# Dispatch of several experts' tokens in one product on split rows, in two groups of places

## The chip, the cores and the metric

The kernel runs on one core of one Trainium2 chip. The metric is the device time of one execution in microseconds (us). TensorE is called PE in the profile, VectorE DVE, ScalarE ACT, GpSimd POOL, SyncE SP.

## What is computed

Two transformer blocks in float32 on a sequence of 256 tokens with 1024 features. The change lies in the last layer of the second block, a mixture of experts: a router picks 2 of 8 experts for each token, each expert is a gated network with 3584 hidden features, and the results are weighted and added to their tokens.

```python
D_MODEL = 1024; SEQ = 256; N_EXPERTS = 8; TOP_K = 2; EXPERT_FF = 7 * D_MODEL // 2

def swiglu(h, w_gate, w_up, w_down):
    return (jax.nn.silu(h @ w_gate) * (h @ w_up)) @ w_down

def moe_swiglu(h, w_router, w_gate, w_up, w_down):
    xt = h.reshape(-1, D)
    logits = (xt @ w_router).astype(jnp.float32)
    top_logit, top_idx = lax.top_k(logits, TOP_K)
    gates = jax.nn.softmax(top_logit, axis=-1)
    ...
    xs = xt_pad[tok_buf].reshape(n_blocks, EXPERT_BLOCK, D)
    def expert_block(args):
        xb, e = args
        return swiglu(xb, w_gate[e], w_up[e], w_down[e])
    ys = lax.map(expert_block, (xs, block_expert)).reshape(rows, D)
    ys = ys * gate_buf[:, None].astype(ys.dtype)
    out = jnp.zeros((T + 1, D), ys.dtype).at[tok_buf].add(ys)[:T]
```

## The kernel before

Everything ahead of the experts' layer (attention, convolution, two feed-forward networks) takes the first 753 us and is the same code in both kernels. Dense products there split a float32 operand into two rounded parts of type fp32r, high and low (H and L; `evac_hl`: ACT copies the rounded part, DVE subtracts it from the source), and multiply part by part.

In the experts' layer the 8 places e = 0 to 7 are worked one after the other. Which expert takes which place is decided on the chip by its count of tokens (`places`); places 1, 4 and 7 (`SMALL`) hold up to 64 tokens, the others (`MID`) up to 96 (`CAP`). A place goes through 7 steps d. `gate_up` multiplies the tokens' features (32 or 64 columns of the array, plain float32) with four pieces of weights of 1 MB, `turn` makes silu(gate) times up on ACT and DVE and transposes it on PE (tile `hT`), and `down` multiplies it with two more pieces of 1 MB. `gu` and `gv` are the banks of gate_up, `yb` those of down. Weights come in one stream over SP's DMA queue into a ring of buffers: 8 `raw`, 4 `more0` to `more3` (`EXTRA`), one of two 512 KB halves (`more`, `gn`) and six of two halves (`late`), 19 pieces of 1 MB. A buffer is asked for again as soon as PE has read it (`done`, `issue`).

The tokens of a place are gathered by a product, `dispatch(e)`: `one_hot` writes for each half t of the 256 tokens a 128x128 matrix (token against slot) into the tile `co`, and for each of the 8 blocks of 128 features the normalised rows `z` (tile `xTL`, plain float32) are the stationary operand and the one-hot the moving one, CAP columns wide (64 or 96). Four blocks share a bank `ga`, and ACT copies it to `plain(e)` (tile `xTH`). `back(e)` transposes the one-hot for `combine`, which scatters the results later. Place 0 is dispatched ahead of the loop, from the slots that the router's chain on DVE has just made; the other places in steps that are pushed between weight products: `under` runs one step of the list `aside` at the third and the sixth of the eight blocks of a `gate_up`. `prepare(e + 1)` joins the list after `gate_up` of d = 4. Within these rules a scheduler orders the instructions of each engine.

Of the kernel before, what the change touches and what calls it, by code (L numbers as in the profile page):

```python
# [15 lines left out]
D = 1024  # L16
# [84 lines left out]
EXTRA = 4  # L101
# [15 lines left out]
def build(tc, ap, dbg=None):  # L117
# [1113 lines left out]
    with tc.tile_pool(name="moe", bufs=1) as p:  # L1231
        z = zt
        pad(p, "moe")
        ex = [wide(tag, F32R, E_OFF).rearrange("p (i c s) -> p i c s", i=2, c=8) for tag in ("xTH", "xTL")]
        for i in range(EXTRA):
            issue([p.tile([128, HALF], F32, name="more%d" % i, tag="more%d" % i)])
        pl = wide("xTH", F32)
# [14 lines left out]
        def plain(e):  # L1252

            return pl[:, e % 2 * 768:e % 2 * 768 + 8 * CAP[e]].rearrange("p (c s) -> p c s", c=8)
# [12 lines left out]
        def dispatch(e):  # L1267
            n = CAP[e]
            per = 4
            for b in range(8 // per):  # L1270
                ps = mmbank("ga")
                for i in range(per):
                    cs = slice((per * b + i) * 128, (per * b + i + 1) * 128)
# [3 lines left out]
                o = slice(per * b, per * b + per)  # L1277
                psv = ps[:, 0:per * n].rearrange("p (c s) -> p c s", c=per)
                if e in SMALL + MID:
                    nc.scalar.activation(out=plain(e)[:, o, :], in_=psv, func=AF.Copy)  # L1280
                else:
                    evac_hl(ex[e % 2][:, 0, o, :], ex[e % 2][:, 1, o, :], psv)
                yield
# [9 lines left out]
        def flat(e):  # L1293
            return [ex[e % 2][:, i].rearrange("p c s -> p (c s)") for i in range(2)]

        def combine(e, yb, OHT):
            yH, yL = flat(e)
            n = 128
            if e in SMALL:

                evac_hl(yH[:, 0:512], yL[:, 0:512], yb[0])
            elif e in MID:
                n = CAP[e]
                y = p.tile([128, D], F32, name="y", tag="y", bufs=1)
# [9 lines left out]
            else:  # L1314
                for h in range(2):
                    cs = slice(h * 512, (h + 1) * 512)
                    evac_hl(yH[:, cs], yL[:, cs], yb[h])
# [15 lines left out]

        warm(AF.Silu, rsz[:, 1:2])
        one_hot(0)
        drain(dispatch(0))
# [72 lines left out]
        def prepare(e):  # L1409
            one_hot(e)  # L1410
            yield
            yield from dispatch(e)
            ohts[e] = back(e)
            yield

        def first():
            ohts[0] = back(0)
            yield
            gates()
            yield  # L1420
            places()
            yield

        def hidden(e, d, dt, i=0):

            n = CAP[e]
            if d == 6:
                w = pl[:, 1536:] if dt is F32 else flat(e)[i]
                return w[:, 0:4 * n].rearrange("p (c s) -> p c s", c=4)
            return p.tile([128, 4, 128], dt, name=("hH", "hL")[i], tag=("hH", "hL")[i], bufs=1)[:, :, 0:n]  # L1430

# [4 lines left out]
        def gate_up(e, d, pc):  # L1436
            n = CAP[e]
            if n == 128:
                eH, eL = ex[e % 2][:, 0], ex[e % 2][:, 1]
                ps = [mmbank("gu") for _ in range(2)]  # L1440
                for k8 in range(8):
                    for c in range(2):
                        if 2 * k8 + c in (UG, UG + 7):
                            under()
                        wh, wl = pc(k8 * 1024 + c * 512, 512)
                        mm3(ps[c], eH[:, k8, :], eL[:, k8, :], wh, wl, k8 == 0, k8 == 7)
                return ps
# [27 lines left out]
        def turn_of(e, d, ps, hs):  # L1475

            n = CAP[e]
            if n == 128:
                ss_ = [sb[:, c] for c in range(2)]
                for c in range(2):  # L1480
                    gated(ps[c], ss_[c], 256)
            else:
                ss_ = [sb[:, 0]]
                gated(ps[0], ss_[0], 256)
                if n == 96:
                    ss_.append(sb[:, 1, 0:128])
                    gated(ps[1], ss_[1], 128)

            def turn():
# [6 lines left out]
                if n == 128:  # L1496
                    hH, hL = hidden(e, d, F32R), hidden(e, d, F32R, 1)
                    evac_hl(hH, hL, hT.rearrange("p (c s) -> p c s", c=4))
                    hs[d] = (hH, hL)
                    return  # L1500
                h = hidden(e, d, F32)
# [12 lines left out]
        def down(e, d, pc, h, yb):  # L1514
            n = CAP[e]
            if n == 128:
                hH, hL = h
                order = [(kt, c) for kt in range(4) for c in range(2)]
                if d == 6:
                    order.sort(key=lambda o: o[1])  # L1520
                for m, (kt, c) in enumerate(order):
                    if m == UD:
                        under(0)
                    wh, wl = pc(kt * 1024 + c * 512, 512)
                    mm3(yb[c], hH[:, kt, :], hL[:, kt, :], wh, wl, d == 0 and kt == 0, d == 6 and kt == 3)
                return
# [40 lines left out]
        def overflow(e, beyond):  # L1567
# [11 lines left out]
            y = m[:, D:2 * D]  # L1579
            for b in range(2):  # L1580
                ps = mmbank("ga")
                for i in range(4):
                    cs = slice((4 * b + i) * 128, (4 * b + i + 1) * 128)
                    for t in range(2):
                        nc.tensor.matmul(ps[:, i * 128:(i + 1) * 128], z[:, t, cs], OH[:, t, :], start=t == 0,
                                         stop=t == 1)
                nc.vector.tensor_copy(out=eo[:, 4 * b:4 * b + 4, :], in_=ps.rearrange("p (c s) -> p c s", c=4))
            yb = [accbank("yb") for _ in range(2)]
            for d in range(7):
# [15 lines left out]
                hs_ = p.tile([128, 4, 128], F32, name="hso", tag="hH", bufs=1)  # L1605
# [9 lines left out]
            for h in range(2):  # L1615
                nc.scalar.activation(out=y[:, h * 512:(h + 1) * 512], in_=yb[h], func=AF.Copy)
            for t in range(2):
                for h in range(2):
                    cs = slice(h * 512, (h + 1) * 512)
                    ps = mmbank("cb")  # L1620
                    nc.tensor.matmul(ps, OHT[:, t * 128:(t + 1) * 128].bitcast(F32), y[:, cs], start=True, stop=True)
# [171 lines left out]
```

## Time and profile before

| | us |
|---|---|
| median of 3 runs | 1624.11 |
| lowest and highest run | 1623.15, 1629.3 |
| the profiled execution, its own time | 1626.53 |
| its span in the trace | 1624.5 |

The profile shows the profiled execution alone. Its own time is 2.0 us over its span and 2.4 us over the median of the runs. An engine's busy time is the union of its instructions; matmuls overlap, so the spacing of their starts tells their cost, not the duration of one. A plain float32 matmul leaves two records in the trace, an fp32r matmul one.

### The profile page before, as it was taken

How to read it: one execution, taken by the hardware profiler on the slowest of the kernel's cores; microseconds unless marked ns; L12 is line 12 of the kernel's file. 1: busy time of each engine (PE TensorE's matmuls, PEld its weight loads, DVE VectorE, ACT ScalarE, POOL GpSimd, SP SyncE). 2: the span in 40 equal slices, each digit the busy share in tenths (PEclk: the TensorE clock that was granted, in tenths of full speed). 3: DMA queues.
4: the chain of work that ended last, by engine and by line, in shares of the span. 5: the costliest groups of instructions: out<-in, count | busy, mean ns of one | idle time of the engine just before them, and what ended most of it. 6: DMA issues, size and time to landing. Idle time of an engine off the chain costs nothing.

```text
span 1624.5 us, 30626 instructions
## 1 busy us (share of the span) xinstructions
PE 1581.2 (97%) x12854; PEld 961.9 (59%) x12854; DVE 613.0 (38%) x1206; ACT 479.9 (30%) x879; POOL 21.9 (1%) x36
## 2 busy tenths in 40 slices
PE   7999999999999999999999999999999999999997
PEld 5879998877899998775343333443433334434332
DVE  6776555678555557972201011011011010110111
ACT  6655444667644446651101000010010000100100
POOL 0000000000000000010000000000000000000000
PEclk9999999999999999999999999999999999999999
DMA  9555555541555555238999999999999999999993
GB/s 380 217 191 201 189 198 182 194 156 53 182 202 187 182 182 195 69 137 340 415 380 374 416 416 414 415 417 401 379 370 415 418 418 415 415 388 387 357 417 127
DMA packets 86132, 478.81 MB, mean 295 GB/s; under 512 B 9761, under 2 KB 10529, under 8 KB 44770
## 3 DMA queue, kind: packets, MB, share of 16 engines
q1 hardware_dynamic: 83312, 468.58, 74.4%
q0 software_dynamic: 2240, 7.60, 1.4%
q8 instruction: 103, 1.69, 0.4%
q10 hardware_dynamic: 434, 0.59, 0.1%
q14 instruction: 43, 0.35, 0.1%
HBM read 475.03 MB, written 1.05 MB: 293 GB/s over the span
## 4 chain that ended last, share of the span: by engine, by line
PE 91%; DVE 5%; ACT 2%; issue 1%; DMA 0%; POOL 0%; SPq 0%; DVEq 0%; ACTq 0%; POOLq 0%
PE gu L1459 24%; PE yb L1534 12%; PE gv L1463 7%; PE acc L276 4%; PE acc L274 4%; PE acc L275 4%; PE yb L1539 4%; PE mm L276 3%; PE mm L274 3%; PE mm L275 2%; PE ga L1275 2%; PE hT L1494 2%; PE mm L297 2%; PE mm L296 2%; PE mm L295 2%; PE pg L297 1%
## 5 line engine op out<-in xcount | busy, mean ns | idle before, releaser
L226 DVE TENSOR_TENSOR wl<-raw,wh 128x1024 fp32r<-128x1024 f32 (+1 forms) x240 | 265.3, 1115 | 156.3 <-ACT wh L225 152.0
L225 ACT ACTIVATE wh<-raw 128x1024 fp32r<-128x1024 f32 (+1 forms) x240 | 230.8, 972 | 175.6 <-PE acc L276 64.1
L1459 PE MATMUL gu<-raw,xTH 128*32 128x512 f32 (+1 forms) x1240 | 190.0, 594 | 0.0
L1472 ACT ACTIVATE sm<-gu 128x256 f32<-128x256 f32 x56 | 21.5, 384 | 538.9 <-PE gu L1459 538.9
L1473 DVE TENSOR_TENSOR sm<-sm,gu 128x256 f32<-128x256 f32 x56 | 23.6, 421 | 384.4 <-ACT sm L1472 384.4
L1459 PE MATMUL gu<-late,xTH 128*32 128x512 f32 (+1 forms) x880 | 135.4, 595 | 0.0
L1459 PE MATMUL gu<-more,xTH 128*32 128x512 f32 (+1 forms) x708 | 107.6, 594 | 0.0
L1459 PEld LDWEIGHTS gu<-raw,xTH 128*32 128x32 f32 (+1 forms) x1240 | 49.6, 116 | 61.6 <-issue 42.4
L276 PE MATMUL acc<-wh,fL 128*128 128x512 f32 x216 | 84.6, 392 | 0.0
L275 PE MATMUL acc<-wl,fH 128*128 128x512 f32 x216 | 84.6, 392 | 0.0
L274 PE MATMUL acc<-wh,fH 128*128 128x512 f32 x216 | 84.6, 392 | 0.0
L274 PE MATMUL mm<-wh,xTH 128*128 128x512 f32 (+1 forms) x224 | 82.1, 366 | 2.4 <-ACT xTH L312 2.4
L276 PE MATMUL mm<-wh,xTL 128*128 128x512 f32 (+1 forms) x224 | 80.5, 360 | 1.9 <-DVE xTL L313 1.9
L1534 PE MATMUL yb<-raw,hH 128*32 128x512 f32 (+1 forms) x536 | 80.6, 596 | 0.0
L275 PE MATMUL mm<-wl,xTH 128*128 128x512 f32 (+1 forms) x224 | 79.6, 356 | 0.0
L1463 PE MATMUL gv<-raw,xTH 128*32 128x256 f32 x944 | 72.5, 379 | 0.0
L1463 PEld LDWEIGHTS gv<-raw,xTH 128*32 128x32 f32 x944 | 30.7, 110 | 70.6 <-issue 70.3
L1507 DVE COPY hH<-hT 128x128 f32<-128x128 f32 x60 | 14.6, 286 | 132.9 <-PE yb L1539 120.4
L1534 PE MATMUL yb<-late,hH 128*32 128x512 f32 (+1 forms) x400 | 62.7, 596 | 0.0
L295 PE MATMUL mm<-xTH,wh 128*128 128x256 f32 x224 | 62.7, 280 | 0.0
L296 PE MATMUL mm<-xTL,wh 128*128 128x256 f32 x224 | 62.5, 279 | 0.0
L297 PE MATMUL mm<-xTH,wl 128*128 128x256 f32 x224 | 62.5, 279 | 0.0
(384 smaller groups left out, 2751.9 us busy)
## 6 DMA issues: line engine op xcount, KB each, us to landing
raw<-in_moegu SPq DMA_DIRECT2D x96, 1024.0 KB, 11.4
late<-in_moegu SPq DMA_DIRECT2D x136, 512.0 KB, 10.1
more<-in_moegu SPq DMA_DIRECT2D x48, 1024.0 KB, 11.7
raw<-in_moedn SPq DMA_DIRECT2D x48, 1024.0 KB, 12.1
late<-in_moedn SPq DMA_DIRECT2D x68, 512.0 KB, 10.1
raw<-in_mlp SPq DMA_DIRECT2D x32, 1024.0 KB, 5.1
more<-in_moedn SPq DMA_DIRECT2D x24, 1024.0 KB, 17.5
raw<-in_ffgu SPq DMA_DIRECT2D x22, 1024.0 KB, 5.1
```

Source lines behind the costliest of these rows:

```text
L225: nc.scalar.activation(out=wh[:, cs], in_=src[:, cs], func=AF.Copy)
L226: nc.vector.tensor_tensor(out=wl[:, cs], in0=src[:, cs], in1=wh[:, cs].bitcast(F32), op=OP.subtract)
L274: nc.tensor.matmul(out, aH, bH, start=start, stop=False)
L275: nc.tensor.matmul(out, aH, bL, start=False, stop=False)
L276: nc.tensor.matmul(out, aL, bH, start=False, stop=stop)
L295: nc.tensor.matmul(out, wh, xH[:, k, :], start=k == 0, stop=False)
L296: nc.tensor.matmul(out, wh, xL[:, k, :], start=False, stop=False)
L297: nc.tensor.matmul(out, wl, xH[:, k, :], start=False, stop=k == 7)
L1459: nc.tensor.matmul(ps[0][r:r + w, :], es_[:, k8, g * w:g * w + w], pc.plain(k8 * 1024 + c * 512, 512), start=k8 == 0, stop=k8 == 7)
L1463: nc.tensor.matmul(ps[1][q * 32:q * 32 + 32, 0:256], es_[:, k8, 64:96], pc.plain(k8 * 1024 + q * 256, 256), start=k8 == 0, stop=k8 == 7)
L1534: nc.tensor.matmul(yb[0][r:r + w, :], h[:, kt, g * w:g * w + w], pc.plain(kt * 1024 + c * 512, 512), start=d == 0 and kt == 0, stop=d == 6 ...
L1539: nc.tensor.matmul(yb[1][q * 32:q * 32 + 32, 0:256], h[:, kt, 64:96], pc.plain(kt * 1024 + q * 256, 256), start=d == 0 and kt == 0, stop=d ...
```

## The change

Only place 0 is still gathered by a plain float32 product ahead of the loop. For the other seven, `z` is split once into fp32r parts zH and zL (`halves_of_z`), and one product gathers the tokens of several places at once: the one-hots of places 1, 2, 3 and 7 stand side by side in the tile `ohb`, 320 columns wide, and are the moving operand; zH and zL of both halves of the tokens are the stationary ones, four matmuls for each block of 128 features. A second group holds places 4, 5 and 6, 256 columns. `batch(g)` is pushed in steps of two blocks between the weight products of place 0 and of place 2. ACT copies up to 256 columns of a bank to the group's tile (`esx`, in the room of `z`, or `esy`), DVE the last 64 to `es7`. `one_hot(e)` and `back(e)` stay for every place. The new tiles take the room of `more3`, so that the ring has 18 pieces; `y` and one split tile `yhl` serve all places, and the transposed hidden rows of d = 6 go to `y`. `overflow`, for places with more tokens than they hold, is adapted and is not entered here. Branches for places of 128 slots, which there are none of, go.

```diff
-EXTRA = 4
+EXTRA = 3
+BATCH = ((1, 2, 3, 7), (4, 5, 6))
...
-        def dispatch(e):
-            n = CAP[e]
...
-                        nc.tensor.matmul(ps[:, i * n:(i + 1) * n], z[:, t, cs], OH[:, t, 0:n], start=t == 0,
-                                         stop=t == 1)
...
+        def halves_of_z():
+            for t in range(2):
+                evac_hl(zH[:, t, :], zL[:, t, :], z[:, t, :])
+
+        def batch(g):
+
+            n = 0
+            for e in g:
+                for t in range(2):
+                    nc.vector.tensor_scalar(out=ohb[:, t, n:n + CAP[e]], in0=C("iota")[:, 0:CAP[e]],
+                                            scalar1=vp[:, t, e:e + 1], scalar2=None, op0=OP.is_equal)
+                n += CAP[e]
+            m = min(n, 256)
+            yield
+            for b in range(8):
+                ps = mmbank("ga")
+                cs = slice(b * 128, (b + 1) * 128)
+                for i, (t, zz) in enumerate((t, zz) for t in range(2) for zz in (zH, zL)):
+                    nc.tensor.matmul(ps[:, 0:n], zz[:, t, cs], ohb[:, t, 0:n], start=i == 0, stop=i == 3)
+                to = (esx if g[0] < 4 else esy)[:, b, :]
+                nc.scalar.activation(out=to, in_=ps[:, 0:m], func=AF.Copy)
+                if n > m:
+                    nc.vector.tensor_copy(out=es7[:, b, :], in_=ps[:, m:n])
+                if b % 2:
+                    yield
...
         def prepare(e):
             one_hot(e)
             yield
-            yield from dispatch(e)
             ohts[e] = back(e)
             yield

         def first():
             ohts[0] = back(0)
+            halves_of_z()
             yield
...
                 if e == 0 and d == GC:
                     aside.append(first())
+                if d == GC and e in (0, 2):
+                    aside.append(batch(BATCH[e // 2]))
```

What stands on PE at the end of place 0, in `gate_up` of d = 5 (before): the first half of the dispatch of place 1, between products with the weights.

```order
L1459 MATMUL gu<-more_7433,xTH 32x512 x4
L1463 MATMUL gv<-more_7433,xTH 32x256 x4
L1275 MATMUL ga<-co,xTL 128x64 x8
L1459 MATMUL gu<-more_7433,xTH 32x512 x4
L1463 MATMUL gv<-more_7433,xTH 32x256 x4
```

And now, in `gate_up` of d = 4, a quarter of the first group's product (`xTH` and `xTL` are zH and zL here).

```order
L1474 MATMUL gu<-raw,esy 32x512 x4
L1478 MATMUL gv<-raw,esy 32x256 x4
L1309 MATMUL ga<-ohb,xTH 128x320
L1309 MATMUL ga<-ohb,xTL 128x320
L1309 MATMUL ga<-ohb,xTH 128x320
L1309 MATMUL ga<-ohb,xTL 128x320
L1309 MATMUL ga<-ohb,xTH 128x320
L1309 MATMUL ga<-ohb,xTL 128x320
L1309 MATMUL ga<-ohb,xTH 128x320
L1309 MATMUL ga<-ohb,xTL 128x320
L1474 MATMUL gu<-raw,esy 32x512 x4
L1478 MATMUL gv<-raw,esy 32x256 x4
```

There are 14 halves of dispatches in the loop before, which stand on PE in 22 pieces, since some are broken by weight products; now there are 8 such quarters, each in one piece.

The second place is DVE's chain from the router to the one-hot of place 0 (`co<-co,route`), before, from the write of M of the first half of the tokens on.

```order
L1217 TENSOR_SCALAR M<-route 128x8
L515 TENSOR_TENSOR x<-acc,x 128x512
L1222 SCALAR_TENSOR_TENSOR route<-lgT,M 128x8
L1223 TENSOR_SCALAR route<-route 128x8
L1264 TENSOR_SCALAR co<-co,route 128x128
L1196 COPY xTH<-tp 128x4x128
...
L1217 TENSOR_SCALAR M<-route 128x8
L1344 TENSOR_SCALAR route<-route 128x16
L1345 TENSOR_TENSOR route<-M,route 128x16
L1222 SCALAR_TENSOR_TENSOR route<-lgT,M 128x8
L1347 TENSOR_TENSOR route<-route 128x16
L1223 TENSOR_SCALAR route<-route 128x8
L1264 TENSOR_SCALAR co<-co,route 128x128
```

And now the same stretch; `xTL<-xTL,xTH` is the subtraction for zL.

```order
L1218 TENSOR_SCALAR M<-route 128x8
L516 TENSOR_TENSOR x<-acc,x 128x512
L1223 SCALAR_TENSOR_TENSOR route<-lgT,M 128x8
L314 TENSOR_TENSOR xTL<-xTL,xTH 128x1024
L1224 TENSOR_SCALAR route<-route 128x8
L1197 COPY xTH<-tp 128x4x128
...
L1218 TENSOR_SCALAR M<-route 128x8
L314 TENSOR_TENSOR xTL<-xTL,xTH 128x1024
L1223 SCALAR_TENSOR_TENSOR route<-lgT,M 128x8
L1371 TENSOR_SCALAR route<-route 128x16
L1224 TENSOR_SCALAR route<-route 128x8
L1372 TENSOR_TENSOR route<-M,route 128x16
L1374 TENSOR_TENSOR route<-route 128x16
L1275 TENSOR_SCALAR co<-co,route 128x128
```

The scheduler has moved the two subtractions of `halves_of_z`, which the code writes after the start of the loop, into this chain, each 1024 columns wide and ahead of the operations that make the slots.

On ACT the copies for zH have moved with them: the first stands between the square root and the squares of the second half's rows.

```order
L344 ACTIVATE rsz<-rsz,eps 128x1
L313 ACTIVATE xTH<-xTL 128x1024
L339 ACTIVATE sq,ss<-x 128x512
L344 ACTIVATE rsz<-rsz,eps 128x1
L172 ACT_TABLE_LOAD
L172 ACTIVATE scr<-rsz,eps 128x1
L313 ACTIVATE xTH<-xTL 128x1024
L1288 ACTIVATE esy<-ga 128x384 x2
```

Without the two rows of 128x1024 these are ACT's rows before.

## Rows read from the trace of the kernel before

**Rows 1.** The profiled page: PE's busy time; the chain that ended last, by engine.

```profile
PE 1581.2 (97%) x12854; PEld 961.9 (59%) x12854; DVE 613.0 (38%) x1206; ACT 479.9 (30%) x879; POOL 21.9 (1%) x36
PE 91%; DVE 5%; ACT 2%; issue 1%; DMA 0%; POOL 0%; SPq 0%; DVEq 0%; ACTq 0%; POOLq 0%
```

**Rows 2.** Stretches: PE, PEld, DVE, ACT, POOL busy; granted clock; DMA share; GB/s.

```profile
900.00:925.00 25.00, 24.06 (x114) 7.81 (x111) 2.11 (x5) 1.05 (x3) 0.00 (x0) 1.00 1.02 415
...
1175.00:1200.00 25.00, 25.00 (x297) 10.90 (x293) 2.47 (x10) 1.43 (x4) 0.00 (x0) 1.00 0.92 340
...
1575.00:1600.00 25.00, 23.98 (x114) 7.85 (x110) 2.12 (x5) 0.77 (x2) 0.00 (x0) 1.00 0.75 311
```

**Rows 3.** Place 2's first piece: SP's issue, us to landing, PE's first use.

```profile
920.64 2.49 SPq L216 DMA_DIRECT2D more<-in_moegu  x2
...
more<-in_moegu SPq DMA_DIRECT2D x1, 1024.0 KB, 19.4
...
957.66 1.07 PE L1459 MATMUL gu<-more,xTH 128*32 128x512 f32 x8
```

**Rows 4.** Longest wait of PE for weights, experts' layer: total us, times, longest.

```profile
PEld gu L1459 <- DMA more<-in_moegu: 1.7, 6, 0.4
```

**Rows 5.** PE in order of time, end of place 0: start, duration, operation, records.

```profile
834.70 1.04 PE L1459 MATMUL gu<-more,xTH 128*32 128x512 f32 x8
...
836.10 2.00 PE L1275 MATMUL ga<-co,xTL 128*128 128x64 f32 x16
838.03 1.06 PE L1459 MATMUL gu<-more,xTH 128*32 128x512 f32 x8
...
840.63 1.04 PE L1459 MATMUL gu<-gn,xTH 128*32 128x512 f32 x8
```

**Rows 6.** The same view, place 2: weight products around half a dispatch in four pieces.

```profile
1036.06 1.04 PE L1459 MATMUL gu<-late,xTH 128*32 128x512 f32 x8
...
1044.21 1.06 PE L1459 MATMUL gu<-raw,xTH 128*32 128x512 f32 x8
```

**Rows 7.** PE in order of time, fp32r: eight of 256 columns, three of 512.

```profile
443.20 0.28 PE L295 MATMUL pg<-xTH,wh 128*128 128x256 f32 x1
...
443.99 0.28 PE L296 MATMUL pg<-xTL,wh 128*128 128x256 f32 x1
...
734.62 0.39 PE L275 MATMUL acc<-wl,xTH 128*128 128x512 f32 x1
...
735.08 0.39 PE L274 MATMUL acc<-wh,xTH 128*128 128x512 f32 x1
```

**Rows 8.** PE in order of time, place 3: a transposition right behind its gate_up.

```profile
1152.77 0.55 PE L1494 MATMUL hT<-co,sm 128*128 128x128 f32 x3 [0.53 <-DVE sm L1473]
```

**Rows 9.** DVE in order of time, the chain ahead of the loop.

```profile
742.25 0.69 DVE L1196 COPY xTH<-tp 128x512 f32<-128x512 f32 x1
...
746.31 0.17 DVE L1217 TENSOR_SCALAR M<-route 128x8 bf16<-128x8 f32 x1
...
747.17 0.29 DVE L1264 TENSOR_SCALAR co<-co,route 128x128 f32<-128x128 f32 x1
```

**Rows 10.** Groups by line in the experts' layer: busy us, mean ns, idle before.

```profile
L313 DVE TENSOR_TENSOR xTH<-y,xTH 96x1024 fp32r<-96x1024 f32 x3 | 3.7, 1221 | 4.3 <-ACT xTH L312 4.3
...
L312 ACT ACTIVATE xTH<-y 96x1024 fp32r<-96x1024 f32 x3 | 3.2, 1057 | 0.1
```

**Rows 11.** PE in order of time, ahead of the loop: the convolution's last product; place 0's dispatch.

```profile
740.38 0.39 PE L276 MATMUL acc<-wh,xTL 128*128 128x512 f32 x1
...
747.51 5.97 PE L1275 MATMUL ga<-co,xTL 128*128 128x96 f32 x28 [0.79 <-DVE co L1264]
```

**Rows 12.** Short stretches around place 0's dispatch, columns as in Rows 2.

```profile
747.50:750.50 3.00, 2.99 (x14) 2.99 (x15) 0.00 (x0) 0.00 (x0) 0.00 (x0) 0.50 0.71 262
...
753.50:757.00 3.50, 3.50 (x44) 1.36 (x48) 0.00 (x0) 0.49 (x1) 0.00 (x0) 1.00 1.01 391
```

**Rows 13.** PE in order of time: six plain float32 products of 256 columns.

```profile
705.76 2.86 PE L1136 MATMUL pm<-yc,co 128*128 128x256 f32 x12
```

More of the change, by code (lines that the diff above doesn't have):

```diff
@@ L1233, in build @@
         pad(p, "moe")
-        ex = [wide(tag, F32R, E_OFF).rearrange("p (i c s) -> p i c s", i=2, c=8) for tag in ("xTH", "xTL")]
+        yhl = wide("xTH", F32R, E_OFF)
         for i in range(EXTRA):
             issue([p.tile([128, HALF], F32, name="more%d" % i, tag="more%d" % i)])
-        pl = wide("xTH", F32)
+        zH, zL = (wide(tag, F32R).rearrange("p (t d) -> p t d", t=2) for tag in ("xTH", "xTL"))
+        esx = zt.rearrange("p t d -> p (t d)").rearrange("p (c n) -> p c n", c=8)
+        esy = p.tile([128, 8, 256], F32, name="esy")
+        es7 = p.tile([128, 8, CAP[7]], F32, name="es7")
+        ohb = p.tile([128, 2, 320], F32R, name="ohb")
         issue([xnp.tile([128, PIECE], F32, name="more", tag="xn", bufs=XN), gn])
@@ L1252, in plain @@
         def plain(e):
-            return pl[:, e % 2 * 768:e % 2 * 768 + 8 * CAP[e]].rearrange("p (c s) -> p c s", c=8)
+            if e == 0:
+                return esy.rearrange("p c n -> p (c n)")[:, 0:8 * CAP[0]].rearrange("p (c s) -> p c s", c=8)
+            if e == 7:
+                return es7
+            o = sum(CAP[i] for i in range(1 if e < 4 else 4, e))
+            return (esx if e < 4 else esy)[:, :, o:o + CAP[e]]
         def one_hot(e):
@@ L1265, in one_hot, with dispatch @@
                                             op0=OP.is_equal)
-        def dispatch(e):
-            n = CAP[e]
-            per = 4
-            for b in range(8 // per):
+        def dispatch():
+            n = CAP[0]
+            for b in range(2):
                 ps = mmbank("ga")
-                for i in range(per):
-                    cs = slice((per * b + i) * 128, (per * b + i + 1) * 128)
+                for i in range(4):
+                    cs = slice((4 * b + i) * 128, (4 * b + i + 1) * 128)
                     for t in range(2):
@@ L1276, in dispatch @@
                                          stop=t == 1)
[L1277 to L1283, printed above, removed]
+                nc.scalar.activation(out=plain(0)[:, 4 * b:4 * b + 4, :],
+                                     in_=ps[:, 0:4 * n].rearrange("p (c s) -> p c s", c=4), func=AF.Copy)
+        def halves_of_z():
[21 more added lines that the diff above has]
+                    yield
         def back(e):
@@ L1293, in flat @@
         def flat(e):
-            return [ex[e % 2][:, i].rearrange("p c s -> p (c s)") for i in range(2)]
+            return [yhl[:, i * D:(i + 1) * D] for i in range(2)]
         def combine(e, yb, OHT):
             yH, yL = flat(e)
-            n = 128
             if e in SMALL:
                 evac_hl(yH[:, 0:512], yL[:, 0:512], yb[0])
-            elif e in MID:
+            else:
                 n = CAP[e]
-                y = p.tile([128, D], F32, name="y", tag="y", bufs=1)
                 for g in range(2):
@@ L1422, in first, with hidden @@
             yield
-        def hidden(e, d, dt, i=0):
+        def hidden(e, d):
             n = CAP[e]
             if d == 6:
-                w = pl[:, 1536:] if dt is F32 else flat(e)[i]
-                return w[:, 0:4 * n].rearrange("p (c s) -> p c s", c=4)
-            return p.tile([128, 4, 128], dt, name=("hH", "hL")[i], tag=("hH", "hL")[i], bufs=1)[:, :, 0:n]
+                return y[:, 0:4 * n].rearrange("p (c s) -> p c s", c=4)
+            return p.tile([128, 4, 96], F32, name="h", tag="hH", bufs=1)[:, :, 0:n]
         def gate_up(e, d, pc):
             n = CAP[e]
[L1438 to L1447, printed above, removed]
             es_ = plain(e)
@@ L1477, in turn_of @@
             n = CAP[e]
[L1478 to L1487, printed above, removed]
+            ss_ = [sb[:, 0]]
+            gated(ps[0], ss_[0], 256)
+            if n == 96:
+                ss_.append(sb[:, 1, 0:128])
+                gated(ps[1], ss_[1], 128)
             def turn():
@@ L1495, in turn @@
                         o += 128
[L1496 to L1501, printed above, removed]
+                h = hidden(e, d)
                 if n == 64:
@@ L1515, in down @@
             n = CAP[e]
[L1516 to L1526, printed above, removed]
             for kt in range(4):
@@ L1583, in overflow @@
                     cs = slice((4 * b + i) * 128, (4 * b + i + 1) * 128)
[L1584 to L1586 removed]
+                    for m, (t, zz) in enumerate((t, zz) for t in range(2) for zz in (zH, zL)):
+                        nc.tensor.matmul(ps[:, i * 128:(i + 1) * 128], zz[:, t, cs].bitcast(F32), OH[:, t, :],
+                                         start=m == 0, stop=m == 3)
                 nc.vector.tensor_copy(out=eo[:, 4 * b:4 * b + 4, :], in_=ps.rearrange("p (c s) -> p c s", c=4))
```

15 lines of the change are left out of this document (6 added, 9 removed).

## The prediction

> **What bounds the kernel now.** I read the page first. PE is busy 97% of the span and makes 91% of the chain that ended last [rows 1], so time leaves the kernel where PE's own work gets shorter. The stretches come next, because the change sits in the experts' layer, from 753 us on: there PE is busy 24 to 25 us of every 25, while DVE and ACT are busy 1 to 6 [rows 2]. The DMA share is near 1 in the same rows, so the weights could be a second bound just behind. They are not yet. While places of 64 slots run, DMA gives its full 415 GB/s; in the places of 96 slots, after 1175 us, it falls to 340 GB/s with PE full, so all buffers are full and DMA waits for PE; the last weights land before 1600 us. The thinnest reserve before the end is at the start of place 2: that piece was issued at 920.6, landed 19.4 us later at 940.0, and PE took it at 957.7, a reserve of 17.6 us [rows 3]. PE's longest total of waits for weights is 1.7 us in 6 waits [rows 4]. So PE's instruction stream sets the time, with 17 us of weights in hand at the worst place.
>
> **Dispatches removed.** One step of gate_up between two block starts takes 1.30 us on PE: from 838.03 to 840.63 are two of them. With half a dispatch in between it takes 834.70 to 838.03, 3.33 us, so the half costs 2.03 [rows 5]. Its 16 records take 2.00 us with the last one's tail of 0.28, so they start 0.115 us apart, and a product (two records) costs 0.23. Eight make 1.84; the remaining 0.2 is paid once for each piece put into the stream of weight products. Half a dispatch of 96 slots in four pieces lengthens four steps by 1044.21 - 1036.06 - 4 x 1.30 = 2.95 us [rows 6]; eight products and four pieces give 2.64, a little low, so the price of a piece lies between 0.2 and 0.28. Places 1 to 7 had 7 x 16 = 112 products in 22 pieces: 112 x 0.23 + 22 x 0.2 = **30.2 us** go.
>
> **Products added.** 32 matmuls of 320 columns and 32 of 256, all fp32r with 128x128 weights. Eight such matmuls of 256 columns start 0.79 us apart from first to last, 0.113 each; three of 512 columns 0.46, 0.23 each [rows 7]. 320 columns are not in the trace: bounds are 0.113 and 0.23; I take 0.142, a straight line between, since the steps of 256 and 512 grow with the columns. That is 32 x 0.113 + 32 x 0.142 = 8.2 us (7.2 to 11.0), and 8 pieces x 0.2 = 1.6. **9.8 us** are added, net **-20.4** (-21.4 to -17.6).
>
> **Order of the turns.** In place 3 the transposition of a `turn` stood right behind its gate_up, and PE idled 0.5 us for DVE's product [rows 8]. It stood so in places 3 and 6 once each in the old order, and nowhere in a 96-slot place in the new one. In the small places ten stand so in either order. I take **-1.0** (0 to -3, if partial waits go too).
>
> **The chain ahead of the loop.** This is where the change costs. The split of `z` was written for the loop, but DVE now does both subtractions inside the chain that makes place 0's one-hot, and PE has nothing else to do then. A subtraction of 1024 columns takes 1.22 us on DVE, ACT's copy ahead of it 1.06 [rows 10]. zH takes over the room of the convolution's high part, so ACT's first copy can start only when PE's last convolution product is done, 740.38 + 0.39 = 740.8 [rows 11]. It ends at 741.9, the subtraction at 743.1, a small operation follows, and the copy of the transposed rows that began at 742.25 begins near 743.35, 1.1 later. M of the second half comes at 746.3 + 1.1 = 747.4 instead of 746.3; the second subtraction then stands ahead of the slots (+1.2), with two more small operations of the gates (+0.2), while 0.3 of it lies in the wait for PE that was there. The one-hot that began at 747.17 [rows 9] begins about 749.4, **2.2 us later**.
>
> What PE loses by that hangs on the clock. Place 0's dispatch ran at a granted clock of 0.50, and from 753.5 on it was 1.00 [rows 12]; its 28 records took 5.97 us, 0.21 each, against 0.115 at full clock [rows 11, 5]. If the clock returns at the moment it returns now, the last third of the dispatch runs at full speed and the loss is about 1.0; if it returns as long after the dispatch began as now, 2.2; every further us at half costs 0.5. I take **+2.0** (1.0 to 4.0).
>
> **What is hidden.** 14 narrow one-hots (at most 0.29 each, as the 128-wide one [rows 9]) and 8 copies to `es7` go to a DVE that has 19 of 25 us free or more; 16 copies to `esx` and `esy` on ACT replace 14. Uncovered they would cost some 6 us on DVE. Two `ga` banks a step, beside `gu` and `gv`, use all four banks; the copies have about 4 us until the next step, and if one is late it costs its own length, 0.4 us, eight times at the most. `y`, `yhl` and the hidden rows share rooms only with work that PE has finished a place earlier. The ring loses one piece, which is 1.05 MB at 415 GB/s = 2.5 us of reserve; the gain of PE in place 1 (one dispatch, 4 us) takes another 4, so about 11 of 17.6 stay. SP is moved past nothing: the issues of a piece keep their place in the stream.
>
> **Sum.** -20.4 - 1.0 + 2.0 = **-19.4 us**. The profiled execution took 1626.53 (span 1624.5 and 2.0 around it), so it would take 1607.1; it lies 2.4 above the median of the runs, 1624.11, and I predict **1604.7** for the median. The bounds add up to -23.4 and -13.6, so 1600.7 to 1610.5; runs vary by a few us, so I widen to 1598 to 1612 for this case. The measurement can tell about 0.5%, 8 us, from no change.
>
> **Rivals.**
>
> The weights take it back. With 18 pieces, a faster PE and DMA that gives no more than 417 GB/s, PE would wait in places 1, 4 and 7. A small place needs 42 pieces x 2.5 = 105 us of DMA and PE is through in 86. For it: DMA is at its limit in those rows [rows 2]. Against it: 17.6 us in hand at the thinnest place [rows 3], refilled in each 96-slot place, where DMA idles (340 of 417 GB/s). It decides when PE gains more than 15 us between full buffers and the end of a small place; the dispatches there are worth 4. Then half the gain or all of it goes: 1614 to 1624.
>
> The split buys nothing. If the merged products ran at the rate of plain float32, they would cost two records of 0.217 us at 256 columns (2.86 us for 12, less the tail [rows 13]), 0.43 a matmul, and 0.54 at 320: 31 us with 1.6 for the pieces instead of 9.8, that is +22.8 on the sum, +3.4 over all: **1627.5**, slower than now. It decides at a mean of 0.4 us for a matmul. Against it: the same type with weights of the same shape runs at 0.113 all over the first 700 us [rows 7].
>
> The old dispatches are cheaper than I read. If a narrow product cost what its columns cost and no more, the 48 of 64 columns and the 64 of 96 would take less than 0.23. The half of 64 columns and that of 96 agree with one price for both [rows 5, 6], which speaks against it: the price does not hang on the columns. The Trainium skill, page FP8 and Floating Point Precision, section TensorE Precision Notes, says that true float32 takes 4 passes through the array. By four passes at 2.4 GHz, as an estimate, 64 columns would take 0.11 us and 96 columns 0.16, the removed work 15.4 + 4.4 = 19.8 instead of 30.2, and the kernel 1615. The trace does not agree, with 0.23 for 64 columns.
>
> A better order. Shape changes and partial waits that I priced at nothing in small places could go too: another -4, 1598 or a little below.
>
> **How the numbers follow.** Forecast 0.84; better order 0.06; weights take it back 0.05; old dispatches cheaper 0.02; split buys nothing 0.03. The predicted time is the forecast's. Its 1598 to 1612 hold 0.84, and nothing more has to be taken in. All of the forecast and the better order end under 1616, with part of the third and fourth cases: faster by over 0.5% 0.93; within 0.5% 0.06 (the rest of those, and most of the split's case); slower 0.01.
>
> **What would show it.** Right: 64 fp32r rows of `ga` 0.11 and 0.14 us apart, in 8 pieces; gate_up of d = 5 and 6 in places 2 to 6 near 10.5 us without a dispatch; the one-hot of place 0 some 2 us later; the thinnest reserve near 11 us. Wrong: PE waiting for `raw` or `late` by more than a few us, `ga` rows waiting for ACT, the clock at 0.50 well into place 0, or the products of 320 columns at 0.23.

## The result, and the profile after

The changed kernel takes **1608.4 us** (median of 4 runs, 1606.1 to 1609.5), the kernel before 1624.8 beside it (4 runs, 1623.2 to 1629.3): a ratio of 0.989, 95% interval 0.987 to 0.991. That is 16.4 us less by the medians and some 18 by the ratio. The forecast was 1604.7, with a range of 1598 to 1612. The profiled execution took 1606.13, its span is 1604.3; that of before was 1624.5.

The first view is the page: busy times, and the chain that ended last, by engine.

```profile
PE 1557.7 (97%) x12694; PEld 942.1 (59%) x12694; DVE 618.3 (39%) x1230; ACT 481.4 (30%) x883; POOL 22.7 (1%) x36
PE 91%; DVE 5%; ACT 2%; DMA 1%; issue 1%; POOL 0%; SPq 0%; ACTq 0%; DVEq 0%; POOLq 0%
```

PE has 160 records fewer and is still 97% of the span and 91% of the chain [rows 1]: the bound is the same, with less work in it.

The merged products next, in PE's order of time: the first piece of the first group (320 columns, with weight products of place 0 around it), then two lines of the second group, of 256 columns.

```profile
833.98 0.61 PE L1478 MATMUL gv<-more,esy 128*32 128x256 f32 x8
834.53 0.41 PE L1309 MATMUL ga<-ohb,xTH 128*128 128x320 f32 x1
834.77 0.31 PE L1309 MATMUL ga<-ohb,xTL 128*128 128x320 f32 x1
834.92 0.31 PE L1309 MATMUL ga<-ohb,xTH 128*128 128x320 f32 x1
...
835.65 0.31 PE L1309 MATMUL ga<-ohb,xTL 128*128 128x320 f32 x1
835.89 1.07 PE L1474 MATMUL gu<-more,esy 128*32 128x512 f32 x8
...
1004.02 0.28 PE L1309 MATMUL ga<-ohb,xTH 128*128 128x256 f32 x1
1004.14 0.28 PE L1309 MATMUL ga<-ohb,xTL 128*128 128x256 f32 x1
```

They start 0.147 us apart at 320 columns and 0.12 at 256. The edges of a piece (an unbroken run of such products between weight products) stand out: its first product comes 0.55 behind the start of a `gv` group, where the next weight product comes after 0.43 otherwise, and is 0.24 ahead of the second; the last is again 0.24 ahead of gate_up. That is some 0.3 that a piece costs beyond its products.

Where the time went is seen best by places: each time is the distance between the first gate_up rows of a place and of the next.

```
place                       0       1       2       3       4       5       6    sum
before                 118.23   86.02  121.36  122.08   87.48  120.75  121.17  777.09
after                  120.46   81.34  122.01  116.15   83.30  116.88  116.16  756.30
before, no dispatch    114.09   81.49  116.26  117.37   82.96  116.55  117.31  746.03
after, no merged prod. 115.90   81.50  116.88  116.16   83.30  116.87  116.16  746.77
```

(The last two lines are of experiments below.) Places 0 and 2 carry the merged products and are no shorter; the others lose 4 to 6 us each. Sum: -20.8.

The chain ahead of the loop, DVE in order of time, then PE's dispatch of place 0 and short stretches (PE, PEld, DVE, ACT, POOL busy; granted clock; DMA share; GB/s).

```profile
738.61 0.15 DVE L1223 SCALAR_TENSOR_TENSOR route<-lgT,M 128x8 f32<-128x8 f32 x1
738.86 1.23 DVE L314 TENSOR_TENSOR xTL<-xTL,xTH 128x1024 fp32r<-128x1024 f32 x1
...
744.21 1.22 DVE L314 TENSOR_TENSOR xTL<-xTL,xTH 128x1024 fp32r<-128x1024 f32 x1
745.34 0.16 DVE L1223 SCALAR_TENSOR_TENSOR route<-lgT,M 128x8 f32<-128x8 f32 x1
745.80 0.28 DVE L1275 TENSOR_SCALAR co<-co,route 128x128 f32<-128x128 f32 x1
```

```profile
746.13 6.29 PE L1286 MATMUL ga<-co,xTL 128*128 128x96 f32 x28 [1.58 <-DVE co L1275]
752.35 1.41 PE L1474 MATMUL gu<-raw,esy 128*32 128x512 f32 x8
```

```profile
742.80:753.00 10.20, 7.07 (x34) 6.36 (x37) 3.10 (x14) 2.04 (x3) 0.00 (x0) 0.50 0.83 261
753.20:757.00 3.80, 3.80 (x52) 1.39 (x48) 0.00 (x0) 0.00 (x0) 0.00 (x0) 1.00 1.01 403
```

Both subtractions stand where they were forecast. From DVE's first small operation on `lgT` to place 0's one-hot it is 7.19 us, and to the first gate_up 13.74. In before the same operation and the first gate_up are these rows:

```profile
741.42 0.16 DVE L1222 SCALAR_TENSOR_TENSOR route<-lgT,M 128x8 f32<-128x8 f32 x1
753.41 1.07 PE L1459 MATMUL gu<-raw,xTH 128*32 128x512 f32 x8
```

From there to the one-hot of 747.17 [rows 9] it is 5.75, and to the first gate_up 11.99: the chain costs **1.75**. PE's wait for the one-hot is 1.58, where it was 0.79 [rows 11]. The clock is at 0.50 from 742.8 to 753.1, for 10.2 us; in before it stood there for 6.8, also until 753.0 (at 0.50 in the first and 1.00 in the second stretch of [rows 12]).

The weights: the first piece of place 2 and the last piece of all (its second half's issue, us to landing, PE's first use of the piece), and three stretches of 25 us.

```profile
928.69 0.33 SPq L217 DMA_DIRECT2D late<-in_moegu  x1
late<-in_moegu SPq DMA_DIRECT2D x1, 512.0 KB, 15.0
954.15 1.06 PE L1474 MATMUL gu<-late,xTL 128*32 128x512 f32 x8
1565.29 0.33 SPq L217 DMA_DIRECT2D gn<-in_moedn  x1
gn<-in_moedn SPq DMA_DIRECT2D x1, 512.0 KB, 17.2
1589.61 1.03 PE L1528 MATMUL yb<-more,y 128*64 128x512 f32 x4
```

```profile
900.00:925.00 25.00, 25.00 (x118) 8.23 (x116) 2.11 (x5) 1.15 (x3) 0.00 (x0) 1.00 1.02 419
1175.00:1200.00 25.00, 25.00 (x247) 9.35 (x241) 4.34 (x11) 4.46 (x8) 0.00 (x0) 1.00 1.01 398
1575.00:1600.00 25.00, 17.01 (x80) 5.45 (x76) 4.69 (x8) 0.98 (x2) 0.00 (x0) 0.92 0.28 107
```

928.69 + 15.0 = 943.7 and use at 954.15: 10.5 us in hand at place 2, where there were 17.6 [rows 3]. At the end the second half of the last piece is issued at 1565.29 and lands 17.2 later at 1582.5, and PE takes the piece at 1589.6: **7.1**, against 16.2 before. (A piece of two halves counts as landed with its second half.) In the stretch where DMA idled at 340 GB/s [rows 2] it now moves 398. DMA has come much closer to being the bound, but nowhere binds.

Ahead of the experts the profiled run was 2.8 us faster, where nothing was changed: in before the granted clock stood at 0.50 for 3.4 us near 437 and again near 686, here never. The dips are not all of it: the profile of a later experiment (16 pieces, the split held back) has none and comes to the same first small operation at 741.55, as late as before. The twelve profiles of this study have two, one or no such dips there, whatever the kernel; this is not the change's doing.

### The profile page after: what moved, and what is told of

Its sections match the earlier page's. It is cut to its first block, busy times and chain, and to the rows that moved or that the text cites. A ratio compares the mean times of both kernels' runs of the same rounds, so it can differ in the third digit from the quotient of the medians.

```text
span 1604.3 us, 30377 instructions
## 1 busy us (share of the span) xinstructions
PE 1557.7 (97%) x12694; PEld 942.1 (59%) x12694; DVE 618.3 (39%) x1230; ACT 481.4 (30%) x883; POOL 22.7 (1%) x36
## 4 chain that ended last, share of the span: by engine, by line
PE 91%; DVE 5%; ACT 2%; DMA 1%; issue 1%; POOL 0%; SPq 0%; ACTq 0%; DVEq 0%; POOLq 0%
PE gu L1474 24%; PE yb L1528 12%; PE gv L1478 8%; PE acc L275 5%; PE acc L277 5%; PE acc L276 4%; PE yb L1533 4%; PE mm L277 3%; PE mm L275 3%; PE mm L276 2%; PE mm L296 2%; PE mm L297 2%; PE mm L298 2%; PE hT L1504 2%; PE pg L297 1%; PE pg L296 1%
## 5 line engine op out<-in xcount | busy, mean ns | idle before, releaser
L1474 PE MATMUL gu<-raw,esy 128*32 128x512 f32 (+1 forms) x816 | 117.1, 595 | 0.0
L1474 PE MATMUL gu<-raw,xTL 128*32 128x512 f32 (+1 forms) x560 | 83.6, 593 | 0.0
L1474 PE MATMUL gu<-late,esy 128*32 128x512 f32 (+1 forms) x512 | 73.4, 594 | 0.0
L1512 DVE COPY h<-hT 128x128 f32<-128x128 f32 x60 | 14.6, 286 | 131.7 <-PE yb L1533 119.0
L1528 PE MATMUL yb<-late,h 128*32 128x512 f32 (+1 forms) x416 | 64.8, 596 | 0.0
L1528 PE MATMUL yb<-more,h 128*32 128x512 f32 (+1 forms) x416 | 64.0, 596 | 0.0
L1528 PE MATMUL yb<-raw,h 128*32 128x512 f32 (+1 forms) x416 | 64.0, 596 | 0.0
L296 PE MATMUL pg<-xTH,wh 128*128 128x256 f32 x208 | 58.3, 280 | 0.0
L297 PE MATMUL pg<-xTL,wh 128*128 128x256 f32 x208 | 57.8, 278 | 0.0
## 6 DMA issues: line engine op xcount, KB each, us to landing
raw<-in_moedn SPq DMA_DIRECT2D x38, 1024.0 KB, 13.7
```

What stands on the lines that cost most here:

```text
L296: nc.tensor.matmul(out, wh, xH[:, k, :], start=k == 0, stop=False)
L297: nc.tensor.matmul(out, wh, xL[:, k, :], start=False, stop=False)
L1474: nc.tensor.matmul(ps[0][r:r + w, :], es_[:, k8, g * w:g * w + w], pc.plain(k8 * 1024 + c * 512, 512), start=k8 == 0, stop=k8 == 7)
L1528: nc.tensor.matmul(yb[0][r:r + w, :], h[:, kt, g * w:g * w + w], pc.plain(kt * 1024 + c * 512, 512), start=d == 0 and kt == 0, stop=d == 6 ...
```

## The experiments

Unless said otherwise the edit is to the changed kernel; medians compare with its 1608.4 and with before's, which was run again beside the experiments (1624.6 to 1625.5).

**The dispatches left out of the kernel before** (the copies behind them read `z`):

```
-                ps = mmbank("ga")
-                for i in range(per):
+                ps = z[:, b, :]
+                if e == 0:
+                    ps = mmbank("ga")
+                for i in range(per if e == 0 else 0):
```

> The kernel before, without the dispatch products of places 1 to 7: the copies behind them read z instead of their result, so the experts of places 1 to 7 work on other numbers (the 112 products are left out, everything else is issued as before). Theory (0.23 us a product and 0.2 a piece, whatever the columns): the steps with a dispatch get shorter by 1.9 to 2.2 us for a half of 64 or two pieces of 96, 30 us in all; the time falls by 26 to 30, the rest if any being waits for weights at the end, where the reserve of before, 16.2 us, is less than the 30 gained. Rival (a product of 64 or 96 columns costs what its columns cost in four passes): the steps shrink by two thirds of that, 20 us in all. Second rival (DMA becomes the bound on a wide front): PE waits for weights by 10 us and more, and the time falls by less than 18.

Measured: 1593.6 us, 31.0 less than before (ratio 0.982, 0.980 to 0.983). By places 777.09 - 746.03 = **31.06**, forecast 30.2. Place 0, which held the 64-slot dispatch of place 1, loses 4.14: 2.07 a half. The halves of 96 slots that stand in one piece, in places 1, 2 and 4, lose 2.09 to 2.11: 64 and 96 columns cost the same. No wait for weights is longer than 0.4 us, as in before. The first theory holds; the price by columns (20 us) is out.

**The merged products left out of the changed kernel:**

```
-                ps = mmbank("ga")
...
-                for i, (t, zz) in enumerate(...):
-                    nc.tensor.matmul(ps[:, 0:n], zz[:, t, cs], ohb[:, t, 0:n], start=i == 0, stop=i == 3)
+                ps = z[:, b % 2, :]
```

> The changed kernel without its merged products: the copies behind them read z, so the experts of places 1 to 7 work on other numbers (64 products are left out, the split of z and the one-hots stay). Theory (the added products cost 11.2 us where they stand, and the reserve of weights, 7.1 us at the end, is thinner than that): the steps of places 0 and 2 that hold a piece shrink to 10.32, 11.2 us in all, and PE then waits 2 to 5 us for the weights late in the run, so the time falls by 6 to 11. Rival (DMA is not near): the whole 11.2. Second rival (weights already bind): under 4.

Measured: 1596.8 us, 11.6 less. The four steps that held two pieces each shrink from 13.34, 13.33, 12.88 and 12.89 to 10.32 each: **11.2** in all. (In the table place 0 falls by less, since here the clock was at 0.50 into its first step.) The first rival comes true, the whole 11.2: the thinnest reserve falls to 3.1 us, at the end, and PE still waits for no piece longer than 0.4. So 11.2 us of gain took 4.0 of reserve (in the experiment above, 31 us took 9.6 of before's, from 16.2 to 6.6). My theory of waits took a reserve as spent by the whole gain, though DMA had slack left to refill it: from 1175 to 1200 it moves 419 GB/s here, 398 in the changed kernel.

**Each merged product issued twice** (the gathered rows of places 1 to 7 come out doubled):

```
-                    nc.tensor.matmul(ps[:, 0:n], zz[:, t, cs], ohb[:, t, 0:n], start=i == 0, stop=i == 3)
+                    for r in range(2):
+                        nc.tensor.matmul(..., start=i + r == 0, stop=i == 3 and r == 1)
```

> The changed kernel with each merged product issued twice into the same bank (the gathered rows of places 1 to 7 come out doubled). Theory (a merged product costs its pace, 0.147 us at 320 columns and 0.118 at 256, and a piece of eight some 0.33 more once): each step with a piece grows by 1.18 and 0.94, 8.5 us in all, about 1617. Rival (there is no price of a piece, the 1.51 and 1.28 us that a piece costs are its products' alone): 11.2 us, about 1619.5. My forecast's sum (0.142 and 0.113, 0.2 a piece): 8.2.

Measured: 1616.2 us, +7.8. The steps with two pieces go from 13.34 to 15.68 and from 12.88 to 14.80: 16 products more cost 2.34 and 1.92, **0.146 and 0.12** each, 8.5 in all. So of the 1.51 and 1.28 us that a piece of eight costs, 1.17 and 0.96 are products and **0.33** is the piece. PE in order of time, one piece with its 16 products:

```profile
838.24 0.56 PE L1310 MATMUL ga<-ohb,xTH 128*128 128x320 f32 x2
838.64 0.45 PE L1310 MATMUL ga<-ohb,xTL 128*128 128x320 f32 x2
838.93 0.46 PE L1310 MATMUL ga<-ohb,xTH 128*128 128x320 f32 x2
...
840.40 0.45 PE L1310 MATMUL ga<-ohb,xTL 128*128 128x320 f32 x2
840.78 1.06 PE L1475 MATMUL gu<-more,esy 128*32 128x512 f32 x8
```

Pairs are 0.29 apart, but the first pair takes 0.40: the extra is paid at the piece's edges.

**Merged in plain float32, without the split** (32 products for 64, and no subtraction in the chain; `ohb` is float32 here):

```
...
-                for i, (t, zz) in enumerate((t, zz) for t in range(2) for zz in (zH, zL)):
-                    nc.tensor.matmul(ps[:, 0:n], zz[:, t, cs], ohb[:, t, 0:n], start=i == 0, stop=i == 3)
+                for t in range(2):
+                    nc.tensor.matmul(ps[:, 0:n], z[:, t, cs], ohb[:, t, 0:n], start=t == 0, stop=t == 1)
...
```

> The changed kernel with the merged products taken straight from z and the one-hots in plain float32, without the split of z: 32 matmuls in place of 64, of 320 and 256 columns. Theory (plain float32 costs 0.43 us at 256 columns and 0.54 at 320, so 15.4 us in place of the 8.4 measured; the chain ahead of the loop is 1.8 us shorter): 4 to 6 us slower than the changed kernel, about 1613, still 11 to 13 faster than before. Rival (merging alone makes the gain, the split nothing): within 1 us of the changed kernel or faster by the chain's 1.8. Second rival (my split-buys-nothing case at its price): a mean of 0.4 us a matmul is 12.8 us, 2.6 slower.

Measured: 1611.0 us (ratio to before 0.991, 0.989 to 0.993), 2.6 slower than the changed kernel and 14.5 faster than before. By the profile a step with two pieces takes 15.30 at 320 columns and 14.44 at 256: 7.0 us more in the loop, as the theory has it; the chain falls to 12.09, 1.65 less. That leaves 5; the medians show half of it, and their spread of 5 us in four runs can hold the rest. So most of the gain is the merging, and the split adds 3 to 5. One piece of it, four products (two records each):

```profile
837.50 2.42 PE L1304 MATMUL ga<-ohb,xTL 128*128 128x320 f32 x8
839.85 1.07 PE L1468 MATMUL gu<-more,esy 128*32 128x512 f32 x8
```

**The split held back behind place 0's one-hot**, by a factor of 1.0 that DVE makes from it:

```
+            nc.vector.tensor_scalar(out=one, in0=OH[:, 1, 0:1], scalar1=0.0, scalar2=1.0, op0=OP.mult, op1=OP.add)
...
-                evac_hl(zH[:, t, :], zL[:, t, :], z[:, t, :])
+                nc.scalar.activation(out=zH[:, t, :], in_=z[:, t, :], func=AF.Copy, scale=one)
+                nc.vector.tensor_tensor(out=zL[:, t, :], in0=z[:, t, :], in1=zH[:, t, :].bitcast(F32), op=OP.subtract)
```

> The changed kernel, with the four operations that split z (two ACT copies of 1.06 us, two DVE subtractions of 1.22 us) held back by data until DVE has made place 0's one-hot, so that they lie beside PE's first products of the loop instead of ahead of them. Theory (DVE's chain ahead of the loop is what the added work costs there): the one-hot of place 0 begins 1 to 1.5 us earlier than after's 745.8, the loop starts that much earlier, and the time falls by 1.4 to 2 us against the changed kernel, to about 1606.5. Rival (the granted clock comes back at the same moment whatever the dispatch does, so an earlier dispatch only runs longer at half clock): the loop starts within 0.5 us of where it did. Second rival (the split now comes late for the batch products of place 0): PE waits at the first of them, and the time is the same or longer.

Measured: 1607.2 us (1605.9 to 1610.1), 1.2 less, not to be told from the changed kernel by these runs. The profile shows the mechanism:

```profile
741.93 0.16 DVE L1223 SCALAR_TENSOR_TENSOR route<-lgT,M 128x8 f32<-128x8 f32 x1
747.69 0.29 DVE L1275 TENSOR_SCALAR co<-co,route 128x128 f32<-128x128 f32 x1
749.44 2.36 DVE L1297 TENSOR_TENSOR xTL<-xTL,xTH 128x1024 fp32r<-128x1024 f32 x2 [1.27 <-ACT xTH L1296]
```

The subtractions stand behind the one-hot, which comes 5.76 after the first small operation, as in before, and the loop begins 11.76 after it. Over all the profiles the distance to the loop is 11.75 to 12.3 us in the six kernels without the split in the chain, 12.9 to 14.1 in the six with it: 1.7 in the mean.

**Fewer buffers for the weights**, 16 pieces in flight, and 11, in place of 18:

```
-EXTRA = 3
+EXTRA = 1
```

```
-EXTRA = 3
+EXTRA = 0
...
-            for _ in range(WBUFS // 2):
+            for _ in range(1):
```

> The changed kernel with two of its spare buffers for the experts' weights taken away, 16 pieces of 1.05 MB in flight in place of 18. By the reserve (the time between a piece's landing and PE's first use, 7.1 us at the thinnest, at the end, and 10.5 ahead of place 2; one piece is 2.5 us of transfer at 415 GB/s) the two are 5 us: no change of time, within 1 us, with 2 to 3 us of reserve left. Rival (weights already hold PE back in part, which the changed kernel's waits don't show): slower by 3 to 5 us.

> The changed kernel with seven of its spare buffers for weights taken away, 11 pieces in flight in place of 18: 17.5 us of reserve by 2.5 us a piece, where 7.1 to 12 stand. Theory (reserve is what keeps the weights from being the second bound): PE waits for DMA at the starts of places 2, 4 or 5 and at the end, about 6, 6 and 10 us: slower than the changed kernel by 10 to 22 us, 1618 to 1630. Rival (in flight pieces don't matter, since DMA moves its full rate anyway): within 2 us.

Measured: **1605.1 us** with 16 (1603.8 to 1606.1), no slower but 3.3 faster, and **1624.5** with 11 (1620.5 to 1626.7; ratio to before 0.999): 16 us slower, the whole gain gone. With 16 the first piece of place 2 is issued at 931.95 and lands 16.2 later; PE takes it at 953.02, a reserve of 4.9 in place of 10.5. At the end 0.2 us are left. With 11 the reserve is used up: PE's weight loads wait for their pieces, here around the start of place 2 (us in total, times, longest).

```profile
PEld gu L1474 <- DMA raw<-in_moegu: 4.4, 3, 1.5
PEld yb L1528 <- DMA raw<-in_moedn: 2.1, 2, 1.3
```

```profile
945.75 1.94 PE L1474 MATMUL gu<-raw,xTL 128*64 128x512 f32 x8 [0.66 <-DMA raw<-in_moegu]
948.22 1.94 PE L1474 MATMUL gu<-raw,xTL 128*64 128x512 f32 x8 [0.54 <-DMA raw<-in_moegu]
...
963.24 1.07 PE L1474 MATMUL gu<-raw,xTL 128*32 128x512 f32 x8 [0.64 <-DMA raw<-in_moegu]
```

Place 1 takes 87.2 us in place of 81.3, place 4 89.2 for 83.3. So the rival that the weights take it back is real: it sets in somewhere between 16 and 11 pieces, and the changed kernel has 18.

By the profiles, which differ by 2.35 us, what makes 16 faster is not the weights: the order of the turns came out another way (places 1 and 2 and place 7's steps take 2.2 less, places 4 to 6 1.4 more), the clock at the loop's start cost 0.3 less, and the end is 1.2 shorter. The rest is within the scatter of the runs, some 2 us.

**The end.** From DVE's last operation to the end of the span it is 6.3 us in before and 8.0 in the changed kernel, with the same work in it.

```
-        def store():
+        pad = p.tile([1, 16], F32, name="pad")
+        for i in range(8):
+            nc.sync.dma_start(pad[:, i:i + 1], ap["norm_mix"][0][i:i + 1].rearrange("(a b) -> a b", a=1))
+        def store():
```

> The changed kernel with eight loads of four bytes each on SP's queue, into a tile that nothing reads, ahead of the stores: SP's instructions after them stand some places later. In the changed kernel and in five kernels made from it the span goes on for 8.0 to 8.1 us after DVE's last operation, in the kernel before and in three others for 6.3 to 6.8. The difference is a gap of 2.2 to 2.3 us on SP behind the first or second instruction after its last branch, in one of them with all four stores landed 2.4 us before the gap's end. Theory (the gap hangs on where SP's code lies behind the branch): the gap goes, 6.3 to 6.8 from DVE's last operation to the end, 1.2 to 1.7 less. Rival (it hangs on the number of buffers in the ring, or on the stores): 8.0 as in the changed kernel. The Trainium skill, page Runtime: NRT & Kernel Launch, section Instruction fetch mechanics, says that a taken branch whose target is not in the window of fetched code stalls for a fetch, and that code comes in blocks of 256 instructions; by that a target just ahead of a block's end would stall twice.

Measured: 1607.1 us (1604.8 to 1607.7), 1.35 less, which is within the scatter of the runs; in the profile 6.65 from DVE's last operation to the end. The waits of SP's queue behind its last branch (total, times, longest), of the changed kernel, then of this one:

```profile
SPq L1630 <- SPq L1630: 5.8, 2, 3.5
```

```profile
SPq L1634 <- SPq L1634: 3.7, 2, 3.4
```

Of two idle times on SP one is all but gone with eight instructions ahead of it that nothing waits for. That fits a gap that hangs on where SP's code lies; these eight are loads, though, and instructions without a transfer were not tried. The Trainium skill, page Runtime: NRT & Kernel Launch, section Instruction fetch mechanics, has a reason (a taken branch out of the fetched window stalls, code comes in blocks); that the gap is a second fetch was not seen itself.

**Two combinations**: the split held back with 16 pieces, and the split held back with the eight loads.

> The changed kernel with both edits that looked better in their profiles: the split of z held back until DVE has made place 0's one-hot, and 16 pieces of weights in flight in place of 18 (whose turns fell in a better order). Theory (the two add up: 2.0 in the chain ahead of the loop, 2.5 in the turns and the end): 1603 to 1605, 3.5 to 5.5 faster than the changed kernel. Rival (the order of the turns hangs on the whole program and falls back): 1606 to 1607.

> The changed kernel with both the split of z held back until DVE has made place 0's one-hot and the eight small loads on SP's queue ahead of the stores, with the ring of 18 pieces as it is. Theory (2.0 us in the chain ahead of the loop and 1.2 to 1.7 at the end, which add up): 1604.7 to 1605.2, 3.2 to 3.7 faster than the changed kernel, as good as the kernel with 16 pieces and the held-back split. Rival (the end stays as it is): 1606.4 to 1607.

Measured: **1605.0** (1604.7 to 1605.4) and **1606.6** (1604.4 to 1607.7). The first is the best version here, 19.6 below before, but 0.1 below 16 pieces alone; the second is 0.4 below the eight loads alone. Together with the experiment on the split alone, holding it back gave 1.2, 0.1 and 0.4: most of the chain's 1.7 does not show in the medians. In the second's profile one sees how it can get lost: its one-hot was as early, but the clock stayed at 0.50 into place 0.

```profile
747.50:753.00 5.50, 5.26 (x25) 5.26 (x25) 2.70 (x4) 2.68 (x3) 0.00 (x0) 0.50 0.93 289
753.00:757.50 4.50, 4.50 (x29) 1.91 (x32) 0.00 (x0) 0.49 (x1) 0.00 (x0) 0.50 1.00 385
```

## Why the prediction was right, and where it was off

The direction and the mechanism held: PE's stream sets the time, and what leaves it leaves the kernel. By the steps of the prediction, each against the two profiles:

- **Dispatches removed**: -30.2 forecast, -31.06 shown. One price for 64 and 96 columns holds, but not its two parts: inside a piece the records start 0.112 us apart in before, not 0.115 (which took in the wider first distance), so a product costs 0.224, and a piece some 0.28 beyond its products at 64 columns and 0.31 at 96, not 0.2 (112 x 0.224 + 22 x 0.28 = 31.2).
- **Products added**: +9.8 forecast, **+11.2** shown. The paces were near (0.142 and 0.113 taken, 0.146 and 0.12 measured). The mis-sized term is the piece: 0.2 taken from that reading of the dispatches, 0.33 measured; eight of them and the paces make 1.4.
- **Order of the turns**: -1.0 forecast. 777.09 - 31.06 + 11.16 = 757.19, and the changed kernel has 756.30, with 0.34 lost to the clock in its first step: -1.2. PE's idle time for DVE's product fell from 10.5 us in 12 waits to 9.4 in 10. The two experiments without gathering products agree: the places take 746.03 in the old order and 746.77 in the new, of which 1.81 are the first step at half speed (11.96 for 10.15 us between its first and last start), so the new order is 1.07 shorter. What makes the order was not tested.
- **The chain**: +2.0 forecast, +1.75 in this pair, 1.7 in the mean of the profiles. The one-hot was 1.44 later, not 2.2; PE's dispatch took the rest, with its records at 0.22 us. That the sum came near is in part luck: both parts were off, and other profiles divide it otherwise. With the products issued twice and with the eight loads the one-hot was 2.25 and 2.3 later, as forecast, but the granted clock was back at 1.00 while the dispatch still ran, which took 5.4 us in place of 6.2, and the loop began no later (13.76 us). The medians show 0.1 to 1.2 of this term.
- **Reserve**: "near 11 us" forecast as the thinnest. Place 2 had 10.5, but the thinnest was 7.1, at the end, a place that I had not worked out.
- **What was left out**: the end of the program, +1.7, which the sum took as unchanged, without a reason given.

Together: -31.06 + 11.16 - 1.2 + 0.34 + 1.75 + 1.7 = -17.3, where I had -19.4; the profiles' spans differ by 20.2, of which 2.8 lie ahead of the experts. The measured ratio gives 18, the medians 16.4. So the errors of the single terms, up to 1.7 us, have both signs and leave 2.1 in the sum. The forecast of 1604.7 is 3.7 below the median: 2.1 by these terms, 0.7 since before's median came out at 1624.8, not 1624.1, and the rest is within the scatter of four runs.

Of the rivals, the weights' was the one to watch, and the runs with fewer buffers show that it exists. The split-buys-nothing case is refuted by the pace: it needed a mean of 0.4 us a product, and 0.146 and 0.12 were measured. The old-dispatches case fell with the 31 us.

The float32 version also shows why merging pays. Its plain products cost (15.30 - 10.32) / 2 - 0.33 = 2.16 us for four at 320 columns, 0.54 each, and 0.43 at 256, as their spacing inside a piece does (two records 0.269 and 0.216 apart); the narrow ones of 64 and 96 columns cost 0.22 to 0.23 both. So the wide products here pay for their columns, and from 96 to 64 columns nothing is saved. What sets the narrow price was not tested. The Trainium skill, page FP8 and Floating Point Precision, section TensorE Precision Notes, gives true float32 four passes: by that, as an estimate at 2.4 GHz, 0.53 us at 320 columns and 0.43 at 256, with which the runs agree, and 0.11 at 64, with which they don't.

What stays open: which of the turns' orders a program gets, and why; what sets the price of a narrow product; and whether the gap at the end is a fetch.

## What to carry to other kernels

Narrow products with full-size weights cost here by their number, not by their columns (the same at 64 and at 96): gather several small operands behind one wide moving operand before trying another number type, and put the products in as few places of a tiled stream as the banks allow. When PE gets faster, work out the weights' reserve (landing to first use) at every place where it runs down, the last one too; it shows how near DMA is to taking over. A gain uses up only a part of it where DMA has slack left (here 4.0 of reserve for 11.2 us). Work that is meant for a busy loop but has its inputs early may be scheduled as early as it can run, and land in a serial chain ahead of the loop; look for it there.

## What the runs showed of the hardware

- A plain float32 product with 128x128 weights took 0.22 to 0.23 us at 64 and at 96 columns (inside a piece its two records start 0.112 apart), 0.43 at 256 and 0.54 at 320; an fp32r product 0.12 at 256 and 0.146 at 320.
- A piece of full-array products inside the stream of 32-column tiles cost 0.33 us beyond its products.
- The half-speed stretch around place 0's dispatch was 6.8 us long in six profiles, 10.2 in five and 13.7 in one. It was 10.2 or more in five of the six with the split in the chain and in one of the six without, which speaks for a part of the chain in it; alone it does not decide. In four profiles it outlived the dispatch; place 0's first step then took 0.3 us more twice, and 1.7 and 1.8 more once each.
- With eight loads ahead of SP's last branch the end of the kernel was 1.4 us shorter in the profile.
